# A Strassen down projection whose first two results reach x by a ScalarE copy and a transfer, with norm combinations split later and transposes moved

## The chip, the cores and the metric

The kernel runs on one core of one Trainium2 chip. The metric is device microseconds of that core. The kernel before takes 1888.84 us (median of 3 runs, 1888.61 to 1888.88).

## The reference, cut to what matters

A trunk of two layers on a float32 x of 512 positions by 1024 channels:

```
def swiglu(h, w_gu, w_down):                       # w_gu 1024 x 2*2816, w_down 2816 x 1024
    g, u = jnp.split(h @ w_gu, 2, axis=-1)
    return (jax.nn.silu(g) * u) @ w_down

for l in range(2):
    x = x + 0.5 * swiglu(rmsnorm(x, ln_ffn1[l]), w_ffn1_gu[l], w_ffn1_down[l])
    h = rmsnorm(x, ln_mix[l])
    z = h @ w_in[l]                                # pool input, q, k, v, gate logits
    a = pool_mixer(...) @ w_pool_branch[l]
    b = sliding_window_attention(...) @ w_attn_branch[l]
    x = x + (sigmoid(gp) * a + sigmoid(ga) * b) @ w_out[l]
    x = x + 0.5 * swiglu(rmsnorm(x, ln_ffn2[l]), w_ffn2_gu[l], w_ffn2_down[l])
```

All of it is float32. The change lies in the four SwiGLU blocks and at their borders to the mixers.

## The kernel before, in words

**Precision.** A float32 operand is split in two parts of a rounded type that TensorE takes at full rate: the high part is a copy by ScalarE, the low part is the operand less the high one, by VectorE. A product is then three matmuls (high by high, high by low, low by high). So every weight and every activation needs one pass of ScalarE and one of VectorE before TensorE can use it. `split` does both at once. `halve` issues the copy at once and leaves the subtraction on a list, `unsettled`, which the next call of `settle` issues.

**Strassen.** The products of an FFN are cut in 2 by 2 blocks and computed as seven products instead of eight, in the order a11, s1, s2, a12, s3, s4, a22 (`ORDER`). Three PSUM tiles hold the results, called by their role: a11, s2, s3 and a22 accumulate one upon the other in A, s1 and s4 in C, a12 in Dd. After each product a step reads what has accumulated so far. The factors of s1 to s4 are sums and differences: of weights they are made in SBUF, or by a second DMA that accumulates (issued by GpSimd, so on the queue that the page calls POOL's; the first DMA is issued by SyncE); of activations they are made by VectorE.

**FFN.** The 2816 hidden channels are worked off in three groups: 768 (2 x 384), 1024 and 1024 (2 x 512) in the very first FFN, with the 768 in the middle in the other three. A group is two `block`s (gate and up projection, i = 0 and 1, of width n) and one `down` (back to 1024 channels, added into x). That makes 12 downs. The last of each FFN is called final; with three of the four a norm `nxt` follows, and the last one of all writes the output. A product in a block or a 512-wide down is 24 matmuls in four quarters (c, q) of six, c the weight tile, q one of two row tiles. In a 384-wide down the second weight tile has half the matmuls, 18 in all.

**Order of the work.** All engines are wrapped so that each one's queue is the order in which the program was written (`InOrder`); nothing is scheduled by a planner. What goes between the quarters of a product is written in a dictionary `mid`: the entry (kind, c, q) runs after that quarter, behind a `settle`. After the first weight tile and after each product's step comes `W.prep`, which issues on VectorE and ScalarE the low part, sum and high part of the weights some 3 or 4 tiles ahead (tiles `wl`, `sums`, `wh`, from 7 buffers `raw`) and the loads that have become possible.

**Down.** Each step adds its share into a quarter of x, by a VectorE operation that reads PSUM: two row halves by two column halves (`add(t, d, c)`). The shares of a11 and a12 go into the same quarter, as do those of s1 and s3, and of s2 and s4. The operands of the next products are made between: `high(name)` is ScalarE's copy, `low(name)` VectorE's subtraction, `ops["t4"]` a combination of the last block's transposed result, still in PSUM, with the tile `fa`; fa is then the source of a22's operand. `flush` issues the transposes of the last block's result. In a final down `whole` has ScalarE sum the squares of the x that is complete, and `nxt.feed(q, i, bank)` has TensorE transpose a quarter of x and ScalarE scale it and take its high part.

**Norm.** For the FFN that follows, the class `Norm` makes the factors of the Strassen block from the transposed x: `t1` to `t4` are the combinations (tiles `more` in the trace, `xgh` and `xgl` where they share the place of the plain parts), each a VectorE operation on 128x512 and then a `split`. What isn't done by the end of the producer is kept on a list (`left`, `pend`), and `due` issues one of its steps in a hook of the first block of the FFN: t3 twice, t2 twice, feed(2) and feed(3), t3_split twice, t4 twice. A norm for the mixer (`halves` false) has only the feeds.

**Mixer.** Its first work is `begun`: two tiles `late` (PSUM) take the first half of the first two weight tiles' terms, then after a `settle` the feeds that were left and the q, k, v products follow.

The hooks of an FFN's first block, before:

```
mid = {at: due for at in (
    ("a11", 0, 0), ("a11", 0, 1), ("s1", 0, 0), ("s1", 0, 1), ("a12", 0, 0), ("a12", 0, 1),
    ("s3", 0, 1), ("s3", 1, 1),
)}
mid["s1", 1, 1] = lambda: due(turn[:, 0, :])
mid["s2", 0, 1] = lambda: due(roles[2][:, 0, :])
```

Of the kernel before, what the change touches and what calls it, by code (L numbers as in the profile page):

```python
# [13 lines left out]
AF = mybir.ActivationFunctionType  # L14
ALU = mybir.AluOpType
# [5 lines left out]
S = 512  # L21
# [87 lines left out]
def trunk(ctx, tc, x0, xT, consts, vecs, rows, w_g4, w_g3, w_d8, w_d6, w_qkv, w_u, w_pool, w_gate, w_br, w_out, out):  # L109
# [204 lines left out]
    def term(pt, i, n, wh, wl, ah, al):  # L314
        nc.tensor.matmul(pt, wh, ah, start=i == 0, stop=False)
        nc.tensor.matmul(pt, wh, al, start=False, stop=False)
        nc.tensor.matmul(pt, wl, ah, start=False, stop=i == n - 1)
# [30 lines left out]
    class Norm:  # L348
# [61 lines left out]
        def t1(self, j):  # L410
            d = temp("d")
            nc.vector.tensor_tensor(out=d, in0=self.keep[0, j], in1=self.keep[1, j], op=ALU.subtract)
            split(*self.both(T1, j), d)

        def t3(self, j):
            self.keep[4, j] = t = self.place(1, 2, j, F32)
# [2 lines left out]
        def t2(self, j):  # L419
            t = self.keep[0, j]  # L420
            nc.vector.scalar_tensor_tensor(
                out=t, in0=t, scalar=-1.0, in1=self.keep[4, j], op0=ALU.mult, op1=ALU.subtract
            )
            split(*self.both(T2, j), t)

        def t3_split(self, j):
            split(*self.both(T3, j), self.keep[4, j])

        def t4(self, j):
            u = temp("t4")  # L430
            nc.vector.scalar_tensor_tensor(
                out=u, in0=self.keep[0, j], scalar=-1.0, in1=self.keep[3, j], op0=ALU.mult, op1=ALU.subtract
            )
            split(*self.both(T4, j), u)

        def first(self, j, src, scale):
            d = temp("d")[:, :HT]
# [80 lines left out]
    def due(bank=None):  # L518
        if pend:
            pend.pop(0)(bank)  # L520
# [9 lines left out]
    def ffn(ctx, nm, nxt, last):  # L530
# [129 lines left out]
        def low(name):  # L660
            ops.pop((name, "low"))()
# [103 lines left out]
        def down(n, final):  # L765

            jn = n // P

            def add(t, d, c):
                def go(pt):  # L770
                    y = x[:, 2 * t:2 * t + 2, d * S:(d + 1) * S]
                    nc.vector.scalar_tensor_tensor(out=y, in0=pt, scalar=c, in1=y, op0=ALU.mult, op1=ALU.add)
                return go

            def whole(t, d, qs=range(2)):
                if not final:
                    return
                for q in qs:
                    b = 2 * t + q
                    if last:  # L780
                        nc.sync.dma_start(
                            out=out[b * P:(b + 1) * P, d * S:(d + 1) * S], in_=x[:, b, d * S:(d + 1) * S]
                        )
                    else:
                        nxt.squares(d, b)

            def a11(pt):
                add(0, 0, 0.5)(pt)
                return flush

            def s1(pt):
                add(1, 1, -0.5)(pt)
                nc.vector.tensor_tensor(out=f["b"], in0=f["c"], in1=f["b"], op=ALU.subtract)

            def s2(pt):
                add(1, 0, 0.5)(pt)
                low("s3")

            def a12(pt):
                add(0, 0, 0.5)(pt)  # L800
                ops.pop("t4")()
                whole(0, 0)

            def s3(pt):
                add(1, 1, -0.5)(pt)
                low("a22")
                whole(1, 1)

            def s4(pt):
                add(1, 0, 0.5)(pt)  # L810
                whole(1, 0)
                if final:
                    W.sums = None

            def a22(pt):
                y = x[:, 0:2, S:2 * S]
                for q in range(2):
                    nc.vector.scalar_tensor_tensor(
                        out=y[:, q, :], in0=pt[:, q, :], scalar=-0.5, in1=y[:, q, :], op0=ALU.mult, op1=ALU.add
                    )  # L820
                    whole(0, 1, [q])

            mid = {
                ("a11", 1, 0): lambda: low("s2"), ("s1", 0, 1): lambda: low("a12"),
                ("s2", 0, 1): lambda: high("s3", f["b"], n), ("a12", 0, 1): lambda: high("s4", f["c"], n),
                ("s3", 0, 0): lambda: low("s4"), ("s3", 0, 1): lambda: high("a22", f["a"], n),
            }
            if final and nxt is not None:
                spot = [t[:, 0, :] for t in (roles[2], turn)]
                feed = lambda q, t, at: lambda: nxt.feed(q, t, spot[at])  # L830
                mid.update({
                    ("s3", 1, 0): feed(0, 0, 0), ("s3", 1, 1): feed(1, 0, 1), ("s4", 0, 1): feed(2, 1, 0),
                    ("s4", 1, 1): feed(3, 1, 1), ("a22", 0, 1): feed(0, 1, 0), ("a22", 1, 0): feed(1, 1, 1),
                })
                if nxt.halves:
                    mid["a22", 1, 1] = lambda: [nxt.t1(j) for j in range(2)]
                left(nxt)

            strassen(
                ORDER, S, (2, jn - 2), lambda kind, k, q: [ops[kind][:, i, q, k * P:(k + 1) * P] for i in range(2)],  # L840
                dict(a11=a11, s1=s1, s2=s2, a12=a12, s3=s3, s4=s4, a22=a22), mid,
            )

# [5 lines left out]
        for gi, (_, group) in enumerate(groups(nm is first)):  # L849
            for i, n in enumerate(group):  # L850
                if nm is first and gi == i == 0:
                    plain(n, xt, acc, later)
                else:
                    mid = {}
                    if nm is first:
                        if gi == 0:
                            mid["s1", 1, 1] = flush
                    elif gi == i == 0:
                        mid = {at: due for at in (
                            ("a11", 0, 0), ("a11", 0, 1), ("s1", 0, 0), ("s1", 0, 1), ("a12", 0, 0), ("a12", 0, 1),  # L860
                            ("s3", 0, 1), ("s3", 1, 1),
                        )}
                        mid["s1", 1, 1] = lambda: due(turn[:, 0, :])
                        mid["s2", 0, 1] = lambda: due(roles[2][:, 0, :])
                    block(n, i, ORDER, mid)
            down(n, gi == 2)

    @with_exitstack
    def mix(ctx, l, nm, nxt):
# [225 lines left out]
        late = [mm() for _ in range(2)]  # L1095
        w = [W.take("u") for _ in range(2)]

        def begun(h):
            for i in range(2):
                for k, t in enumerate(nm.terms(w[i])[4 * h:4 * h + 4]):  # L1100
                    term(late[i], 4 * h + k, KT, *t)
                if h:
                    W.prep()

        begun(0)
        settle()
        due(side_bank[0])
        for q, width in ((False, 256), (True, 512)):
            pts = [t[:, :width] for t in (mm(), mm(), wide[:, 0, :], wide[:, 1, :])]
            per = CH // width  # L1110
            for c in range(KT // per):
                w_ = W.take("qkv")
                for b in range(NB):
                    for k in range(per):
                        kt, cols = per * c + k, slice(k * width, (k + 1) * width)
                        rows = slice(b % 2 * P, (b % 2 + 1) * P)
                        term(
                            pts[b], kt, KT, *(t[:, kt // 2, b // 2, kt % 2, rows] for t in (nm.h, nm.l)),
                            w_[0][:, cols], w_[1][:, cols],
                        )  # L1120
                    if not q and c == 0 and b == 1:
                        settle()
                        due(side_bank[1])
                    if not q and c == 1 and b == 1:
                        nm.spread(side_bank[1])
                        for i in range(2):
                            pooled(i, late[i])
                if not q and c == 0:
                    settle()
                    nm.sums()  # L1130
                    praw = temp("praw")
                    nc.sync.dma_start(out=praw, in_=w_pool[l])
                    begun(1)
                if c + 1 < KT // per:
                    W.prep()
                if q and c == 1:
                    side(-2)
            for b in range(NB):
                nc.scalar.activation(
                    out=(qs[b] if q else kv[:, b]).rearrange("p h d -> p (h d)"),  # L1140
                    in_=pts[b], func=AF.Copy, scale=nm.rstd[:, b:b + 1],
                )
            W.prep()
            if not q:
                split(*spare[4], praw)
            side(-1 if q else -3)
# [196 lines left out]
```

## Time and profile before

| | |
|---|---|
| runs, median (lowest to highest) | 1888.84 us (1888.61 to 1888.88) |
| profiled execution | 1888.9 us, span 1887.0 us |
| TensorE busy | 1858.3 us, 98% |
| VectorE / ScalarE / GpSimd busy | 1448.5 / 1008.6 / 124.5 us |
| granted TensorE clock | 0.999 |
| DMA, mean over the span | 155 GB/s |

The profile page is one execution. The span runs from its first to its last recorded instruction; the profiled execution's time is slightly longer. PE is TensorE's matmul side, PEld its weight loads, DVE VectorE, ACT ScalarE, POOL GpSimd, SP SyncE. A row of a listing by instruction gives the start in us, the duration, the engine, the line, the operation, output and input by the program's names, the shapes, and in brackets how long the engine had been idle before it and what it had been waiting for. `mm` is a PSUM tile of results, `pt` the PSUM tile of transposed results, `op` an operand of a down, `xg`, `xgh` and `xgl` the scaled transposed x and its parts, `r`, `p`, `u`, `fa`, `fb`, `fc` intermediate results of a block. Since the wrapper records every operation, nearly all have line 97; they are told apart by tiles.

### The profile page before, as it was taken

The numbers are of one execution on the slowest core, as the hardware profiler recorded it, in microseconds if no ns is written. First come the engines' busy times: TensorE is split into PE (matmuls) and PEld (weight loads), VectorE is DVE, ScalarE is ACT, GpSimd is POOL, SyncE is SP. The second block draws the span as 40 slices with busy tenths as digits, with TensorE's granted clock in tenths as the row PEclk, the third lists the DMA queues.
The fourth block names the chain that finished last, engine by engine and source line by source line (L and its number), as shares of the span: only waits on it lengthen the run. The fifth ranks groups of instructions, "written<-read, shape, count | busy, mean of one in ns | idle before, by whom it ended". The sixth has DMA issues, their size and how long they took to land.

```text
span 1887.0 us, 23912 instructions
## 1 busy us (share of the span) xinstructions
PE 1858.3 (98%) x8928; PEld 1555.4 (82%) x8928; DVE 1448.5 (77%) x1829; ACT 1008.6 (53%) x1493; POOL 124.5 (7%) x152
## 2 busy tenths in 40 slices
PE   9999999999999999999999999999999999999998
PEld 8888888887788788988878898888877887899887
DVE  7878878677564988887988878786675648888878
ACT  6555455645454654555665555555554446545553
POOL 0100000000000001110001001100000000001000
PEclk9999999999999999999999999999999999999999
DMA  8687666322223676777657667753212237667763
GB/s 251 179 229 180 193 174 171 125 80 77 79 89 101 166 199 161 183 204 188 170 158 196 157 179 206 191 166 107 90 68 90 93 86 203 171 168 184 218 179 100
DMA packets 87571, 292.80 MB, mean 155 GB/s; under 512 B 9856, under 2 KB 10112, under 8 KB 87456
## 3 DMA queue, kind: packets, MB, share of 16 engines
q1 hardware_dynamic: 67104, 223.47, 35.1%
q0 software_dynamic: 20208, 67.78, 20.4%
q8 instruction: 70, 1.15, 0.2%
q14 instruction: 45, 0.37, 0.1%
q10 hardware_dynamic: 144, 0.03, 0.0%
HBM read 289.15 MB, written 2.10 MB: 154 GB/s over the span
## 4 chain that ended last, share of the span: by engine, by line
PE 80%; DVE 12%; ACT 6%; issue 1%; DMA 1%; SPq 0%; DVEq 0%; ACTq 0%
PE mm L97 73%; DVE wl L97 4%; PE sc L97 4%; DVE sums L97 2%; PE pt L97 2%; ACT wh L97 2%; PE pt_pv L97 1%; DVE x L97 1%; DVE more L97 1%; ACT xgh L97 1%; DVE op L97 1%; ACT xg L97 1%; PE pt_tp L97 1%; DVE fa L97 1%; ACT sq L97 1%
## 5 line engine op out<-in xcount | busy, mean ns | idle before, releaser
L97 ACT CAST wh<-raw 128x1024 fp32r<-128x1024 f32 (+3 forms) x443 | 432.9, 988 | 274.9 <-PE mm L97 197.0
L97 DVE TENSOR_TENSOR wl<-raw,wh 128x1024 fp32r<-128x1024 f32 (+3 forms) x443 | 502.2, 1146 | 90.5 <-PE mm L97 57.8
L97 PE MATMUL mm<-wh,op 128*128 128x512 f32 x1232 | 392.1, 394 | 2.4 <-DVE op L97 2.4
L97 PE MATMUL mm<-wh,more 128*128 128x512 f32 (+1 forms) x1104 | 335.2, 374 | 3.8 <-ACT more L97 2.6
L97 PE MATMUL mm<-wl,xgh 128*128 128x512 f32 (+2 forms) x840 | 310.4, 370 | 5.9 <-DVE wl L97 5.6
L97 PE MATMUL mm<-wh,xgh 128*128 128x512 f32 (+2 forms) x840 | 312.2, 372 | 1.3 <-ACT xg L97 0.8
L97 PE MATMUL mm<-wh,xgl 128*128 128x512 f32 (+2 forms) x840 | 309.8, 369 | 0.9 <-DVE xgl L97 0.9
L97 PEld LDWEIGHTS mm<-wh,op 128*128 128x128 f32 x1232 | 230.6, 188 | 52.4 <-DVE op L97 5.8
L97 PE MATMUL mm<-wl,op 128*128 128x512 f32 x616 | 240.3, 390 | 1.6 <-DVE wl L97 1.6
L97 PEld LDWEIGHTS mm<-wh,more 128*128 128x128 f32 x1104 | 204.7, 188 | 36.8 <-ACT more L97 3.3
L97 PE MATMUL mm<-wl,more 128*128 128x512 f32 (+1 forms) x552 | 206.6, 374 | 1.7 <-DVE wl L97 1.7
L97 DVE TENSOR_TENSOR wl<-sums,wh 128x1024 fp32r<-128x1024 f32 (+1 forms) x140 | 159.0, 1137 | 45.0 <-ACT wh L97 28.7
L97 ACT CAST wh<-sums 128x1024 fp32r<-128x1024 f32 (+1 forms) x140 | 136.2, 981 | 95.0 <-DVE sums L97 52.2
L97 PEld LDWEIGHTS mm<-wl,xgh 128*128 128x128 f32 x840 | 157.9, 188 | 31.1 <-DVE wl L97 10.3
L97 PEld LDWEIGHTS mm<-wh,xgh 128*128 128x128 f32 x840 | 157.8, 188 | 23.5 <-ACT xg L97 2.1
L97 PEld LDWEIGHTS mm<-wh,xgl 128*128 128x128 f32 x840 | 157.8, 188 | 23.2 <-DVE xgl L97 2.1
L97 POOL DMA_DIRECT2D raw<-in_w_g x92 | 79.5, 864 | 1325.5 <-DMA raw<-in_w_g 591.6
L97 PEld LDWEIGHTS mm<-wl,op 128*128 128x128 f32 x616 | 115.8, 188 | 26.2 <-DVE wl L97 3.3
L97 PE MATMUL mm<-xgh,wh 128*128 128x512 f32 x320 | 129.4, 404 | 0.4 <-ACT xgh L97 0.4
L97 PE MATMUL mm<-xgl,wh 128*128 128x512 f32 x320 | 125.3, 392 | 0.4 <-DVE xgl L97 0.4
L97 PE MATMUL mm<-xgh,wl 128*128 128x512 f32 x320 | 125.2, 391 | 0.0
L97 PEld LDWEIGHTS mm<-wl,more 128*128 128x128 f32 x552 | 103.6, 188 | 18.5 <-DVE wl L97 3.3
(247 smaller groups left out, 2397.7 us busy)
## 6 DMA issues: line engine op xcount, KB each, us to landing
raw<-in_w_g SPq DMA_DIRECT2D x160, 512.0 KB, 5.0
raw<-in_w_d SPq DMA_DIRECT2D x100, 512.0 KB, 4.5
raw<-in_w_g POOLq DMA_DIRECT2D x64, 512.0 KB, 6.9
raw<-in_w_g SPq DMA_DIRECT2D x77, 384.0 KB, 4.3
raw<-in_w_d POOLq DMA_DIRECT2D x40, 512.0 KB, 5.5
raw<-in_w_gate SPq DMA_DIRECT2D x32, 512.0 KB, 3.2
raw<-in_w_g POOLq DMA_DIRECT2D x28, 384.0 KB, 5.8
raw<-in_w_br SPq DMA_DIRECT2D x16, 512.0 KB, 3.2
```

Of the source, the lines that this page charges most:

```text
L97: return lambda *args, **kw: self.tc.keep_in_program_order(call(*args, **kw))
```

## The change

In every down the shares of a11 and s1 are no longer added into x by VectorE. `aside` has ScalarE copy them out of PSUM, scaled, into an SBUF tile (`p` or `u`, both free at that time), and `gathered` issues a GpSimd DMA that accumulates the tile into x, one in the second quarter of s1 and one in the second quarter of s2. Around that, in the down, the low part of s4's operand moves from the first quarter of s3 into the step of a12, t4 from the step of a12 to the first quarter of s3, a22's high part from the second to the third quarter of s3, and its low part from the step of s3 to the first quarter of s4. In the final downs the feeds move: feed(0, 0) a quarter earlier, feed(2, 1) two quarters later.

In `Norm`, t1, t2, t3_split and t4 end in `halve` in place of `split`. In the first block of an FFN the steps that were due at (s1, 0, 1), (s1, 1, 1) and (s2, 0, 1) come a quarter earlier or more: one at (a11, 1, 0), feed(2) at (s1, 1, 0), feed(3) at (s2, 0, 0). In the mixer the first four terms of both tiles still run before the settle, but in two pieces: terms 0 and 1 of the one tile and of the other, then terms 2 and 3; before, four terms of the one tile were followed by four of the other.

```diff
--- before.py
+++ after.py
@@ -410,7 +410,7 @@
         def t1(self, j):
             d = temp("d")
             nc.vector.tensor_tensor(out=d, in0=self.keep[0, j], in1=self.keep[1, j], op=ALU.subtract)
-            split(*self.both(T1, j), d)
+            halve(*self.both(T1, j), d)
 
         def t3(self, j):
             self.keep[4, j] = t = self.place(1, 2, j, F32)
@@ -421,17 +421,17 @@
             nc.vector.scalar_tensor_tensor(
                 out=t, in0=t, scalar=-1.0, in1=self.keep[4, j], op0=ALU.mult, op1=ALU.subtract
             )
-            split(*self.both(T2, j), t)
+            halve(*self.both(T2, j), t)
 
         def t3_split(self, j):
-            split(*self.both(T3, j), self.keep[4, j])
+            halve(*self.both(T3, j), self.keep[4, j])
 
         def t4(self, j):
             u = temp("t4")
             nc.vector.scalar_tensor_tensor(
                 out=u, in0=self.keep[0, j], scalar=-1.0, in1=self.keep[3, j], op0=ALU.mult, op1=ALU.subtract
             )
-            split(*self.both(T4, j), u)
+            halve(*self.both(T4, j), u)
 
         def first(self, j, src, scale):
             d = temp("d")[:, :HT]
@@ -784,12 +784,23 @@
                     else:
                         nxt.squares(d, b)
 
+            def aside(t, d, c, pt, name):
+                half = wide(name)
+                nc.scalar.activation(out=half, in_=pt, func=AF.Copy, scale=c)
+                pend_x.append((x[:, 2 * t:2 * t + 2, d * S:(d + 1) * S], half))
+
+            def gathered():
+                y, half = pend_x.pop(0)
+                nc.gpsimd.dma_start(out=y, in_=half, accum_op=ALU.add)
+
+            pend_x = []
+
             def a11(pt):
-                add(0, 0, 0.5)(pt)
+                aside(0, 0, 0.5, pt, "p")
                 return flush
 
             def s1(pt):
-                add(1, 1, -0.5)(pt)
+                aside(1, 1, -0.5, pt, "u")
                 nc.vector.tensor_tensor(out=f["b"], in0=f["c"], in1=f["b"], op=ALU.subtract)
 
             def s2(pt):
@@ -798,12 +809,11 @@
 
             def a12(pt):
                 add(0, 0, 0.5)(pt)
-                ops.pop("t4")()
+                low("s4")
                 whole(0, 0)
 
             def s3(pt):
                 add(1, 1, -0.5)(pt)
-                low("a22")
                 whole(1, 1)
 
             def s4(pt):
@@ -821,15 +831,16 @@
                     whole(0, 1, [q])
 
             mid = {
-                ("a11", 1, 0): lambda: low("s2"), ("s1", 0, 1): lambda: low("a12"),
-                ("s2", 0, 1): lambda: high("s3", f["b"], n), ("a12", 0, 1): lambda: high("s4", f["c"], n),
-                ("s3", 0, 0): lambda: low("s4"), ("s3", 0, 1): lambda: high("a22", f["a"], n),
+                ("a11", 1, 0): lambda: low("s2"), ("s1", 0, 1): lambda: [low("a12"), gathered()],
+                ("s2", 0, 1): lambda: [high("s3", f["b"], n), gathered()], ("a12", 0, 1): lambda: high("s4", f["c"], n),
+                ("s3", 0, 0): lambda: ops.pop("t4")(), ("s3", 1, 0): lambda: high("a22", f["a"], n),
+                ("s4", 0, 0): lambda: low("a22"),
             }
             if final and nxt is not None:
                 spot = [t[:, 0, :] for t in (roles[2], turn)]
                 feed = lambda q, t, at: lambda: nxt.feed(q, t, spot[at])
                 mid.update({
-                    ("s3", 1, 0): feed(0, 0, 0), ("s3", 1, 1): feed(1, 0, 1), ("s4", 0, 1): feed(2, 1, 0),
+                    ("s3", 0, 1): feed(0, 0, 0), ("s3", 1, 1): feed(1, 0, 1), ("s4", 1, 0): feed(2, 1, 0),
                     ("s4", 1, 1): feed(3, 1, 1), ("a22", 0, 1): feed(0, 1, 0), ("a22", 1, 0): feed(1, 1, 1),
                 })
                 if nxt.halves:
@@ -857,11 +868,11 @@
                             mid["s1", 1, 1] = flush
                     elif gi == i == 0:
                         mid = {at: due for at in (
-                            ("a11", 0, 0), ("a11", 0, 1), ("s1", 0, 0), ("s1", 0, 1), ("a12", 0, 0), ("a12", 0, 1),
+                            ("a11", 0, 0), ("a11", 0, 1), ("a11", 1, 0), ("s1", 0, 0), ("a12", 0, 0), ("a12", 0, 1),
                             ("s3", 0, 1), ("s3", 1, 1),
                         )}
-                        mid["s1", 1, 1] = lambda: due(turn[:, 0, :])
-                        mid["s2", 0, 1] = lambda: due(roles[2][:, 0, :])
+                        mid["s1", 1, 0] = lambda: due(turn[:, 0, :])
+                        mid["s2", 0, 0] = lambda: due(roles[2][:, 0, :])
                     block(n, i, ORDER, mid)
             down(n, gi == 2)
 
@@ -1095,14 +1106,16 @@
         late = [mm() for _ in range(2)]
         w = [W.take("u") for _ in range(2)]
 
-        def begun(h):
+        def begun(ks):
             for i in range(2):
-                for k, t in enumerate(nm.terms(w[i])[4 * h:4 * h + 4]):
-                    term(late[i], 4 * h + k, KT, *t)
-                if h:
+                terms = nm.terms(w[i])
+                for k in ks:
+                    term(late[i], k, KT, *terms[k])
+                if ks[-1] == KT - 1:
                     W.prep()
 
-        begun(0)
+        begun((0, 1))
+        begun((2, 3))
         settle()
         due(side_bank[0])
         for q, width in ((False, 256), (True, 512)):
@@ -1130,7 +1143,7 @@
                     nm.sums()
                     praw = temp("praw")
                     nc.sync.dma_start(out=praw, in_=w_pool[l])
-                    begun(1)
+                    begun((4, 5, 6, 7))
                 if c + 1 < KT // per:
                     W.prep()
                 if q and c == 1:
```

## The prediction

> **What bounds the kernel now.** I read the cores first, then the busy times, then busy time by stretch, then who waits for whom in the stretches that fall short.
>
> ```profile
> core 0: 1887.0 us, clock 0.999
> ```
> ```profile
> PE 1858.3 (98%) x8928; PEld 1555.4 (82%) x8928; DVE 1448.5 (77%) x1829; ACT 1008.6 (53%) x1493; POOL 124.5 (7%) x152
> ```
>
> TensorE runs at full clock and is busy for all but 28.7 us. That understates its stalls, since a matmul's end is modelled. The weight loads (PEld) are the finer measure. Columns of the next rows: the stretch, its length, then PE, PEld, DVE, ACT and POOL busy (with counts), the clock, the DMA share, GB/s. The first is undisturbed, the second the first block of layer 0's second FFN, the third the last down before layer 1's first FFN with that FFN's first block.
>
> ```profile
> 230.00:240.00 10.00, 10.00 (x46) 8.29 (x45) 4.87 (x4) 6.01 (x6) 0.42 (x2) 1.00 0.75 227
> 609.05:654.80 45.75, 42.50 (x187) 32.63 (x186) 39.77 (x56) 30.74 (x44) 2.66 (x4) 1.00 0.56 150
> 926.95:993.00 66.05, 61.70 (x279) 48.10 (x278) 58.23 (x76) 45.91 (x77) 5.18 (x6) 1.00 0.64 172
> ```
>
> Undisturbed, PEld is busy 0.829 of the time and a 512-wide matmul comes every 10/45 = 0.22 us (0.227 between starts). At that rate the second stretch lost 45.75 - 32.63/0.829 = 6.4 us and the third 66.05 - 48.10/0.829 = 8.0 us. VectorE is busy for 87% of the second. So where TensorE waits, it waits for VectorE and ScalarE queues, which run in program order. Who waits, in the second stretch (total us, times, longest), TensorE first:
>
> ```profile
> PEld mm L97 <- DVE wl L97: 2.9, 4, 0.9
> PEld mm L97 <- ACT more L97: 0.9, 1, 0.9
> PEld mm L97 <- ACT wh L97: 0.8, 1, 0.8
> PEld mm L97 <- DVE xgl L97: 0.7, 1, 0.7
> PEld mm L97 <- ACT xg L97: 0.7, 1, 0.7
> PEld mm L97 <- DVE more L97: 0.7, 2, 0.4
> ```
> ```profile
> DVE more L97 <- ACT more L97: 3.2, 4, 1.1
> ```
>
> The last row is the handle: VectorE, behind with its work, sits idle 3.2 us inside split, waiting for ScalarE's high part before it subtracts the low one.
>
> **The change part by part.**
>
> *The offload.* In each of 12 downs two VectorE adds leave and two ScalarE copies come, plus two accumulating transfers on POOL's queue.
>
> ```profile
> L97 DVE SCALAR_TENSOR_TENSOR x<-mm,x x96: 681/1218/1225, 81.8 to 1883.0; 128x1024 f32<-128x1024 f32 x72, 128x512 f32<-128x512 f32 x24
> ```
> ```profile
> L97 ACT COPY p<-mm x23: 793/1007/1019, 56.9 to 1815.6; 128x1024 f32<-128x1024 f32 x16, 128x768 f32<-128x768 f32 x7
> ```
>
> That is 24 x 1.22 = 29 us off VectorE and 24 x 1.01 = 24 us onto ScalarE (53% busy). What does it bring? VectorE in a 512-wide down, from the add of s2:
>
> ```profile
> 712.20 1.23 DVE L97 SCALAR_TENSOR_TENSOR x<-mm,x 128x1024 f32<-128x1024 f32 x1 [0.81 <-PE mm L97]
> ...
> 719.01 1.22 DVE L97 SCALAR_TENSOR_TENSOR x<-mm,x 128x1024 f32<-128x1024 f32 x1
> 720.15 1.21 DVE L97 SCALAR_TENSOR_TENSOR fa<-fa,pt 128x1024 f32<-128x1024 f32 x1
> 721.28 1.22 DVE L97 TENSOR_TENSOR wl<-sums,wh 128x1024 fp32r<-128x1024 f32 x1
> 722.41 1.22 DVE L97 TENSOR_TENSOR op<-fc,op 128x1024 fp32r<-128x1024 f32 x1
> ```
>
> Before s2's add VectorE already waits 0.81 us for TensorE. The adds taken away lie ahead of that wait, so they lengthen it; all that follows stays where it is. I take 0 us for the offload (ends: 0, and a gain of 2 x 1.22 for a down whose queue is late there). ScalarE's copies stand where it has slack, and bank A is next written one product (24 matmuls, 5.4 us) later; price 0. Without that cover each copy would cost about 1 us.
>
> *s4's low part before t4.* TensorE's stalls at the start of s4, first and last of their kinds:
>
> ```profile
> 98.01 0.19 PEld L97 LDWEIGHTS mm<-wl,op 128*128 128x128 f32 x1 [0.83 <-DVE wl L97]
> 98.88 0.30 PEld L97 LDWEIGHTS mm<-wh,op 128*128 128x128 f32 x2 [0.68 <-DVE op L97]
> ...
> 214.59 0.30 PEld L97 LDWEIGHTS mm<-wh,op 128*128 128x128 f32 x2 [0.61 <-DVE op L97]
> ...
> 1871.56 0.30 PEld L97 LDWEIGHTS mm<-wh,op 128*128 128x128 f32 x2 [0.61 <-DVE op L97]
> ```
>
> Now s4's low part runs directly after a12's add: at 720.2 instead of 722.4, before s4 begins. The weight's wl at 721.28 keeps its place. Five 512-wide downs (214.59 to 1871.56) gain 0.5 each, 2.5 us. In four 384-wide ones (98 to 1756) only the second wait goes, the wl wait stays, and a22's low part, now queued behind one wl more, takes some back: 0.4 each, 1.6 us.
>
> *The final downs' transposes.* feed(2,1) asks for an x that s3's add has not written, because that add is queued behind a low part that waits for ScalarE. From the waits of the last down before layer 1, and of the one before layer 0's mix:
>
> ```profile
> PEld mm L97 <- ACT xgh L97: 1.5, 1, 1.5
> ```
> ```profile
> PEld mm L97 <- ACT xgh L97: 2.1, 2, 1.5
> PEld mm L97 <- DVE xgl L97: 0.8, 2, 0.5
> ```
>
> A quarter product (1.36 us) later, that x is there. What is late next: feed(1) waits about 0.2 us for the t4 that now reads PSUM later, and feed(0,1) about 0.6 us for s4's add. So TensorE leaves the down 1.0 us earlier. ScalarE, saturated there, does not get faster: the mix then waits for its first operand, and begun in four pieces gives it 12 matmuls to do where there were 6. Walking both queues, the 13th matmul of the mix starts 1.15 us earlier. Two such places: 2.3 us.
>
> *Splits into halves, and t2 and the feeds one step earlier,* in three first blocks. VectorE and TensorE in the second stretch:
>
> ```profile
> 622.14 0.19 PEld L97 LDWEIGHTS mm<-wh,more 128*128 128x128 f32 x1 [0.94 <-ACT more L97]
> ...
> 648.66 0.19 PEld L97 LDWEIGHTS mm<-wl,more 128*128 128x128 f32 x1 [0.89 <-DVE wl L97]
> ```
> ```profile
> 634.98 1.29 DVE L97 TENSOR_TENSOR more<-more 128x512 fp32r<-128x512 f32 x2
> 636.18 1.22 DVE L97 TENSOR_TENSOR wl<-raw,wh 128x1024 fp32r<-128x1024 f32 x1
> 637.32 1.22 DVE L97 TENSOR_TENSOR sums<-sums,raw 128x1024 f32<-128x1024 f32 x1
> 638.45 1.22 DVE L97 TENSOR_TENSOR r<-r,mm 128x1024 f32<-128x1024 f32 x1
> ```
>
> The 3.2 us of idling go. Two things come: the low part of feed(2) finds VectorE waiting for ScalarE some 0.6 us longer, and T3's second low part, now done at 634.98, moves behind wl, sums and r's add, 3 x 1.14 = 3.4 us. By my walk it ends at 638.6 when TensorE wants it at 637.3, a new stall of 1.3 us in the second half of s3. T4's two waits vanish behind it, so a22 finds its weights and starts at 646.4, where the old one got going at 648.4 (648.66 less one matmul). Gain 2.1 us, in both second FFNs: 4.2. In the third stretch the queue is late from the start, t1's two waits go as well and TensorE brings 1.0 us along: a22 at 983.4 against 986.8, 3.4 us.
>
> *The new wait.* a12's add must now wait for a transfer issued behind POOL's own weight addition. POOL and VectorE in a 512-wide and a 384-wide down, and the landing of POOL's additions (min, median, max):
>
> ```profile
> 707.61 0.87 POOL L97 DMA_DIRECT2D raw<-in_w_g  x1 [8.10 <-DMA raw<-in_w_g]
> ```
> ```profile
> 804.30 0.87 POOL L97 DMA_DIRECT2D raw<-in_w_g  x1 [2.03 <-DVE wl L97]
> ```
> ```profile
> 813.30 1.22 DVE L97 SCALAR_TENSOR_TENSOR x<-mm,x 128x1024 f32<-128x1024 f32 x1
> ```
> ```profile
> DMA to landing us min/median/max: 4.2/5.9/10.8
> ```
>
> POOL is free at 708.5 and the add is due at 719.0: 10.5 us. In the 384-wide down, 805.2 to 813.3: 8.1 us. A transfer within SBUF does not occur in this trace; the nearest row gives 5.9 us, inside both. Behind a late add everything on VectorE slips one for one. Ends: 0, and at 10.8 us 4 x 2.7 + 4 x 0.3 = 12 us. I take 0.3 for each 384-wide down, 1.2 us.
>
> Sum: 2.5 + 1.6 + 2.3 + 4.2 + 3.4 - 1.2 = 12.8 us, against the profiled execution's 1888.9 us (span 1887.0; median of the runs 1888.84): 1876 us.
>
> A rule that speaks against the change: the Trainium skill, "SBUF — State Buffer", section "SBUF: two separate sides", holds that a DMA issued from GpSimd can starve, since its descriptors are not written while VectorE holds the shared port in a two-port mode. Here POOL's issue took 0.87 us both at 707.61 and at 804.30 with VectorE busy, so this trace does not show it; by the rule the transfers would land late, and the time would be that of the first rival. The same skill's "DMA: Bandwidth & Descriptors", section "Anatomy of one DMA", gives about 2.0 us plus bytes/436e3, an estimate of 3.2 us for 512 KB; the measured median is 5.9. By it the 1.2 us fall away: 1875 us.
>
> **The rivals.**
> *The transfer is late* (slower). If it takes over L us from POOL's turn to land, the cost is 4(L - 8.1) + 4(L - 10.5); it eats the 14.0 us at L = 11.05. At 13 it is 30 us: 1905. For it: two transfers follow each other and weight loads run beside them. Against: the median of 5.9. Final downs have far more time. Chance 0.12, starved descriptors 0.03 of it.
> *The blocks give nothing back:* VectorE, 87% busy, loses at T3 and feed(2) what the splits free. Then 7.6 us go: about 1883.5. For it: my walk leaves 1.3 us of new stall. Against: 3.2 us of idling removed from the late engine. Chance 0.17.
> *The offload does pay:* the queue keeps its lead past s2's add, the wl wait at 98.01 (0.83) goes too and the blocks give a little more: 4 x 0.7 and 3 us more, 1870. Against: the 0.81 us wait at 712.20. Chance 0.11.
>
> **How the numbers follow.** The forecast, 1871 to 1881, has 0.60. The range 1869 to 1886 leaves out the late transfer and little else. A measurement of this kernel can tell about 0.2%, 3.8 us, from no change. Faster by more than that: the forecast, the offload that pays and most of the blocks' case, 0.80; within it 0.09 (the poor end of that case, a transfer slightly late); slower 0.11.
>
> **What would show it.** VectorE's idle time before s2's add should grow beyond 0.81 us; the waits of TensorE for op at s4 should be gone and the 0.83 for wl stay; the 1.5 us at feed(2,1) should be gone; VectorE's waits for ScalarE's more should nearly vanish, with a new TensorE wait for the low part of T3; a12's adds should show no wait for a DMA, or a short one in the 384-wide downs. Transfers that land after 8 to 10 us, or a wait of a12's add above 1 us in every down, would make the prediction wrong.

## The result and the profile after

The changed kernel takes 1876.48 us (median of 4 runs, 1876.08 to 1877.06), the kernel before, beside it, 1888.72 us (1888.13 to 1888.88). The ratio is 0.9936, with a 95% interval of 0.9919 to 0.9953: 12.2 us faster, where 12.8 had been forecast (1876). The profiled execution's span went from 1887.0 to 1874.3 us. First its cores and its busy times:

```profile
core 0: 1874.3 us, clock 1.000
```
```profile
PE 1854.3 (99%) x8928; PEld 1556.8 (83%) x8928; DVE 1421.7 (76%) x1805; ACT 1029.8 (55%) x1517; POOL 152.0 (8%) x176
```

VectorE lost 24 instructions and 27 us, ScalarE gained 24 and 21 us, POOL gained 24 instructions. TensorE has the same 8928 matmuls at the same clock (0.999 before): what went is waiting. Next the two stretches of the prediction, at the same instructions but for the first, which begins 0.4 us earlier here (length, then PE, PEld, DVE, ACT, POOL busy, clock, DMA share, GB/s):

```profile
606.30:650.66 44.36, 42.05 (x190) 33.07 (x189) 40.31 (x57) 30.64 (x44) 3.12 (x4) 1.00 0.58 154
921.95:985.05 63.10, 60.92 (x282) 48.36 (x280) 58.95 (x77) 46.07 (x77) 5.14 (x6) 1.00 0.68 180
```

By the undisturbed rate of 0.829 the first lost 44.36 - 33.07/0.829 = 4.5 us (6.4 before), the second 4.8 (8.0 before). From the block's first weight load to that of the next one, the first block itself went from 45.75 to 43.90 us. Who waits for whom in the first of them, TensorE's rows (total us, times, longest):

```profile
PEld mm L97 <- DVE more L97: 1.7, 2, 1.4
PEld mm L97 <- DVE wl L97: 1.7, 2, 0.9
...
PEld mm L97 <- DVE xgl L97: 0.7, 1, 0.7
PEld mm L97 <- ACT xg L97: 0.6, 1, 0.6
```

The waits for ScalarE's more and wh are gone and there were two fewer waits for wl. VectorE's wait for ScalarE inside split, 3.2 us before, has no row here any more. In its place stands the stall that was forecast at 1.3 us; VectorE's queue, and TensorE at s3's second half:

```profile
634.71 1.21 DVE L97 TENSOR_TENSOR r<-r,mm 128x1024 f32<-128x1024 f32 x1
635.84 0.68 DVE L97 TENSOR_TENSOR more<-more 128x512 fp32r<-128x512 f32 x1
```
```profile
636.57 0.30 PEld L97 LDWEIGHTS mm<-wh,more 128*128 128x128 f32 x2 [1.41 <-DVE more L97]
```

In the downs, VectorE's low part for a12, then its adds of s2 and a12, in a 512-wide one; then the two adds in a 384-wide one:

```profile
700.02 1.23 DVE L97 TENSOR_TENSOR op<-pt,op 128x1024 fp32r<-128x1024 f32 x1 [1.35 <-ACT op L97]
...
708.07 1.23 DVE L97 SCALAR_TENSOR_TENSOR x<-mm,x 128x1024 f32<-128x1024 f32 x1 [1.66 <-PE mm L97]
714.88 1.22 DVE L97 SCALAR_TENSOR_TENSOR x<-mm,x 128x1024 f32<-128x1024 f32 x1
...
803.17 1.23 DVE L97 SCALAR_TENSOR_TENSOR x<-mm,x 128x1024 f32<-128x1024 f32 x1 [0.84 <-PE mm L97]
...
808.65 1.22 DVE L97 SCALAR_TENSOR_TENSOR x<-mm,x 128x1024 f32<-128x1024 f32 x1
```

The wait before s2's add is longer (0.81 to 1.66), and a12's add waits for no transfer in any of the 12 downs. The 0.85 us are not all that was taken away: two adds, 1.14 us each from start to start, have gone from the queue. Most of the rest is the new wait of 1.35 us in the first row, for ScalarE's high part, which now stands behind the copy of a11's share in ScalarE's queue. So ScalarE's copies do hold VectorE up here; the kernel's time does not show it, since VectorE waits for TensorE behind that in any case. TensorE in a 384-wide down and around a final one:

```profile
97.81 0.19 PEld L97 LDWEIGHTS mm<-wl,op 128*128 128x128 f32 x1 [0.83 <-DVE wl L97]
102.41 0.30 PEld L97 LDWEIGHTS mm<-wh,op 128*128 128x128 f32 x2 [0.42 <-DVE op L97]
...
328.32 0.42 PEld L97 LDWEIGHTS mm<-cst,x 128*128 128x128 f32 x4 [0.39 <-DVE x L97]
331.73 0.42 PEld L97 LDWEIGHTS pt<-cst,x 128*128 128x128 f32 x4 [0.40 <-DVE fa L97]
341.73 0.42 PEld L97 LDWEIGHTS mm<-cst,x 128*128 128x128 f32 x4 [0.62 <-ACT xgh L97]
346.09 0.19 PEld L97 LDWEIGHTS mm<-xgl,wh 128*128 128x128 f32 x1 [0.54 <-DVE xgl L97]
```

At s4 the 0.83 for wl stayed, the waits for op are gone (no row in the 512-wide downs either), and TensorE waits 0.42 for a22's low part. The 1.5 us at feed(2, 1) became three small stalls. The transfers, with KB each and median us from issue to landing, and their issues on POOL in the 384-wide down:

```profile
x<-p POOLq DMA_DIRECT2D x12, 512.0 KB, 7.2
x<-u POOLq DMA_DIRECT2D x12, 512.0 KB, 8.6
```
```profile
800.46 1.53 POOL L97 DMA_DIRECT2D x<-p  x1
801.17 2.04 POOL L97 DMA_DIRECT2D x<-u  x1
```

From 800.46 to the add at 808.65 there were 8.2 us of room.

### The profile page after: what moved, and what is told of

The parts are those of the page before. It is cut to its first block, busy times and chain, and to the rows that moved or that the text cites. A ratio compares the mean times of both kernels' runs of the same rounds, so it can differ in the third digit from the quotient of the medians.

```text
span 1874.3 us, 23990 instructions
## 1 busy us (share of the span) xinstructions
PE 1854.3 (99%) x8928; PEld 1556.8 (83%) x8928; DVE 1421.7 (76%) x1805; ACT 1029.8 (55%) x1517; POOL 152.0 (8%) x176
## 4 chain that ended last, share of the span: by engine, by line
PE 84%; DVE 8%; ACT 5%; issue 2%; DMA 1%; SPq 0%; DVEq 0%; POOL 0%; ACTq 0%
PE mm L97 77%; PE sc L97 4%; DVE wl L97 2%; PE pt L97 2%; ACT wh L97 2%; DVE sums L97 1%; PE pt_pv L97 1%; DVE x L97 1%; DVE more L97 1%; ACT sq L97 1%; ACT xgh L97 1%; ACT xg L97 1%; PE pt_tp L97 1%; DVE xgl L97 0%; ACT s L97 0%
```

## The experiments

Twelve kernels, each timed in five rounds beside the kernel before, which took 1888.67 to 1888.89 us there; the changed kernel's 1876.48 is from its own comparison. The runs of one kernel lie within 1.7 us of each other, except where said. Expectations speak of theories by letter: A is always the prediction's way of reckoning, that a stall belongs to the place where an in-order queue is late.

**The four parts, undone one at a time.** First the offload:

```diff
-                aside(0, 0, 0.5, pt, "p")
+                add(0, 0, 0.5)(pt)
...
-                aside(1, 1, -0.5, pt, "u")
+                add(1, 1, -0.5)(pt)
...
-                ("s1", 0, 1): lambda: [low("a12"), gathered()],
-                ("s2", 0, 1): lambda: [high("s3", f["b"], n), gathered()],
+                ("s1", 0, 1): lambda: low("a12"),
+                ("s2", 0, 1): lambda: high("s3", f["b"], n),
```

> The changed kernel, but the shares of a11 and s1 are again added into x by VectorE; no copy by ScalarE, no transfer. Theory A (the prediction: the adds lie ahead of a wait for TensorE, so taking them away only lengthens that wait): same time as the changed kernel, 1876.5 us within 1 us, VectorE's wait before s2's add back from 1.67 to about 0.8 us in 512-wide downs and to 0 in 384-wide ones. Rival B (the offload pays because VectorE's queue keeps a lead through the rest of the down): 3 to 6 us slower than the changed kernel, 1879.5 to 1882.5. Rival C (the transfers cost something): up to 2 us faster than the changed kernel.

1876.09 us (1875.94 to 1876.92): the same as the changed kernel, by its own spread. The offload, as it stands in this change, brings nothing. Its trace has the two waits of the 384-wide down where they were:

```profile
812.29 0.19 PEld L97 LDWEIGHTS mm<-wl,op 128*128 128x128 f32 x1 [0.84 <-DVE wl L97]
816.89 0.30 PEld L97 LDWEIGHTS mm<-wh,op 128*128 128x128 f32 x2 [0.42 <-DVE op L97]
```

Second, the order in the downs:

```diff
                 add(0, 0, 0.5)(pt)
-                low("s4")
+                ops.pop("t4")()
...
                 add(1, 1, -0.5)(pt)
+                low("a22")
...
-                ("s3", 0, 0): lambda: ops.pop("t4")(), ("s3", 1, 0): lambda: high("a22", f["a"], n),
-                ("s4", 0, 0): lambda: low("a22"),
+                ("s3", 0, 0): lambda: low("s4"), ("s3", 0, 1): lambda: high("a22", f["a"], n),
```

(in the final downs a22's high part goes into the hook of feed(0, 0), ahead of it)

> The changed kernel with the old order in the downs: t4 in a12's step, s4's low part in the first quarter of s3, a22's high part in its second quarter, a22's low part in s3's step. Theory A (every stall belongs to its own place, the parts add up): 5 x 0.61 + 4 x 0.68 of waits at the start of s4 come back, 4 x 0.42 of the wait for a22's low part in the 384-wide downs go: 4.1 us slower than the changed kernel, 1880.6. Rival D (the offload's lead lets VectorE reach t4 and s4's low part earlier, so the old order costs nothing any more): 1876.5.

1881.15 us, 4.7 more (4.1 expected). Theory A; D is out, since the offload's lead does not reach s4. The old waits are back, first a 384-wide, then a 512-wide down:

```profile
99.36 0.30 PEld L97 LDWEIGHTS mm<-wh,op 128*128 128x128 f32 x2 [0.68 <-DVE op L97]
214.96 0.30 PEld L97 LDWEIGHTS mm<-wh,op 128*128 128x128 f32 x2 [0.61 <-DVE op L97]
```

Third, the norm: split for halve in t1, t2, t3_split and t4, and the old hooks.

> The changed kernel with the old norm: t1 to t4 with both parts split at once, and the old hooks of the first blocks. Theory A: the three first blocks lose what they gained, 1.6 to 2.1 in each second FFN and some 2.3 before layer 1, about 6 us: 1882.5. Rival E (the blocks are bound by VectorE's total work, and the gain seen there comes from work that arrives earlier because of the rest of the change): under 2 us, below 1878.5.

1883.24 us, 6.8 more (some 6 expected): theory A, the blocks' gain is the norm's own. Fourth, the feeds and begun:

```diff
-                    ("s3", 0, 1): feed(0, 0, 0), ("s3", 1, 1): feed(1, 0, 1), ("s4", 1, 0): feed(2, 1, 0),
+                    ("s3", 1, 0): lambda: [high("a22", f["a"], n), nxt.feed(0, 0, spot[0])], ("s3", 1, 1): feed(1, 0, 1), ("s4", 0, 1): feed(2, 1, 0),
...
-        begun((0, 1))
-        begun((2, 3))
+        begun((0, 1, 2, 3))
```

> The changed kernel with the transposes of the final downs and the start of the mixer in the old places. Theory A: the 1.5 us stall at feed(2, 1) comes back in three downs, and the three small stalls (0.39, 0.40, 0.62) go; net 0.9 us at each of the two places before a mixer and somewhat less before layer 1, where VectorE is the limit: 2 to 2.7 us, 1878.5 to 1879.2. Rival F (ScalarE's and VectorE's queues set the start of the next stage, whatever TensorE does before): 0.5 us or less, 1877.

1879.33 us, 2.9 more, just above the 2 to 2.7 of A; F is out. The four together are -0.4 + 4.7 + 6.8 + 2.9 = 14.0 us for a change worth 12.2: nearly additive. The 1.8 us over, more than the scatter of single runs, mean that some parts are worth more beside the others than alone; which, no run here shows, since no two of the four were undone together.

**Inside the norm's part.** Splits back, new hooks kept, then the old hooks with the halves:

```diff
-            halve(*self.both(T1, j), d)
+            split(*self.both(T1, j), d)
```

(and so in t2, t3_split and t4)

> The changed kernel with t1 to t4 split at once again (VectorE waits for ScalarE's high part each time), but with the new hooks of the first blocks. Theory A (the halves carry the gain, because VectorE's waits of 3.2 us in one block go): most of the 6.8 us that undoing both cost, some 4 us, comes back; less the 1.4 us stall at T3's second low part, which the split puts back ahead of wl: 1878.5 to 1881. Rival G (the earlier hooks carry it): 1876.5 or less, since T3's stall goes and nothing else returns.

1883.23 us. This missed the range that A had given: with splits the earlier hooks are worth nothing, since 1883.24 is what splits with the old hooks take. VectorE's 3.2 us of waiting are back, and TensorE's stalls in layer 0's block changed little but their names (0.57 and 1.07 at T2 where splits with the old hooks have 0.95, 0.43 and 0.19; at a22 0.81 and 0.89, where they have 0.78 and 0.89):

```profile
DVE more L97 <- ACT more L97: 3.2, 4, 1.1
```
```profile
619.50 0.19 PEld L97 LDWEIGHTS mm<-wh,more 128*128 128x128 f32 x1 [0.57 <-ACT wh L97]
620.75 0.19 PEld L97 LDWEIGHTS mm<-wl,more 128*128 128x128 f32 x1 [1.07 <-DVE wl L97]
...
645.48 0.19 PEld L97 LDWEIGHTS mm<-wh,more 128*128 128x128 f32 x1 [0.81 <-ACT wh L97]
646.55 0.19 PEld L97 LDWEIGHTS mm<-wl,more 128*128 128x128 f32 x1 [0.89 <-DVE wl L97]
```

```diff
-                            ("a11", 0, 0), ("a11", 0, 1), ("a11", 1, 0), ("s1", 0, 0), ("a12", 0, 0), ("a12", 0, 1),
+                            ("a11", 0, 0), ("a11", 0, 1), ("s1", 0, 0), ("s1", 0, 1), ("a12", 0, 0), ("a12", 0, 1),
...
-                        mid["s1", 1, 0] = lambda: due(turn[:, 0, :])
-                        mid["s2", 0, 0] = lambda: due(roles[2][:, 0, :])
+                        mid["s1", 1, 1] = lambda: due(turn[:, 0, :])
+                        mid["s2", 0, 1] = lambda: due(roles[2][:, 0, :])
```

> The changed kernel with the old hooks of the first blocks (t2's second, feed(2) and feed(3) a quarter or more later), the halves kept. Theory A (with the queues no longer stopped by the splits, the earlier feeds matter: a12 already waits 0.64 for xg, and a quarter is 1.36): up to 1.4 us in each of three blocks, 1877.5 to 1880.5. Rival L (the hooks are worth nothing, as the two runs with splits, alike to 0.01 us with old and new hooks, suggest): 1876.5 within 0.5.

1879.10 us: with halves the hooks are worth 2.6. T2's two waits return, in place of the 0.78 for wl that the changed kernel has there:

```profile
620.67 0.19 PEld L97 LDWEIGHTS mm<-wh,more 128*128 128x128 f32 x1 [0.94 <-ACT more L97]
621.40 0.30 PEld L97 LDWEIGHTS mm<-wh,more 128*128 128x128 f32 x2 [0.43 <-DVE more L97]
```

So the halves alone bring 1883.24 - 1879.10 = 4.1 us, the hooks on top 2.6; hooks without halves 0. An earlier place in a queue that then stops for another engine gains nothing.

Then the one split whose price the prediction had foreseen:

```diff
         def t3_split(self, j):
-            halve(*self.both(T3, j), self.keep[4, j])
+            split(*self.both(T3, j), self.keep[4, j])
```

> The changed kernel with T3 alone split at once again. Theory A (the new stall of 1.4 us in the second half of s3 is the price of moving T3's second low part behind wl, sums and r's addition, and nothing else waits there): it goes in three first blocks, 4.2 us: 1872.3. Rival K (VectorE has no slack up to a22's weights, so most of the stall comes back as a wait for wl at a22): 0.3 to 0.7 each, 1874.3 to 1875.6.

1875.19 us, 1.3 less, 0.43 for each block: K. The 1.41 us stall is gone, and this one, which the changed kernel has not, stands at a22:

```profile
644.30 0.19 PEld L97 LDWEIGHTS mm<-wl,more 128*128 128x128 f32 x1 [1.10 <-DVE wl L97]
```

**begun alone** (its two lines as above, the feeds kept):

> The changed kernel with the mixer's first eight terms in the old order (four of the one tile, then four of the other). Theory A: the wait for the high part of feed(1, 1), 0.62 before, comes back at both mixers, and the 0.54 for its low part stays: 0.6 each, 1877.7. Rival M (ScalarE's queue sets when the mixer gets going, the order of the terms does not matter): 1876.5.

1878.31 us, 1.8 more, 0.9 at each mixer (0.6 expected). So 1.8 of the 2.9 us of the fourth part are the order of the mixer's terms. The waits at its start, 0.54 alone in the changed kernel, are three:

```profile
346.41 0.19 PEld L97 LDWEIGHTS mm<-xgl,wh 128*128 128x128 f32 x1 [0.54 <-DVE xgl L97]
348.02 0.19 PEld L97 LDWEIGHTS mm<-xgh,wh 128*128 128x128 f32 x1 [0.61 <-ACT xgh L97]
348.74 0.19 PEld L97 LDWEIGHTS mm<-xgl,wh 128*128 128x128 f32 x1 [0.54 <-DVE xgl L97]
```

**The transfer made late.** A copy of one column of p onto itself, by VectorE behind s2's add, holds the first transfer back:

```diff
             def s2(pt):
                 add(1, 0, 0.5)(pt)
+                t = pend_x[0][1][:, 0, 0:1]
+                nc.vector.tensor_copy(out=t, in_=t)
+                gathered(0)
                 low("s3")
...
-                ("s1", 0, 1): lambda: [low("a12"), gathered()],
+                ("s1", 0, 1): lambda: low("a12"),
```

(gathered takes the place in the list that it is to issue, by default the last)

> The changed kernel with the first transfer held back: it is issued only once VectorE has passed s2's add, by a copy of one column of its source onto itself there; the second transfer goes first. Theory A (a late transfer delays a12's add, and everything on VectorE behind it one for one): issued at 709.4 and 804.4 in the downs whose a12 adds now start at 714.9 and 808.7, and landing 7.2 us later (the median of these transfers), it makes a12's add wait 1.7 us in a 512-wide down, 3.0 in a 384-wide one and about 1.5 in a final one; 4 x 6.2 = 25 us, less what stalls behind them absorb: 1892 to 1902. If they land 5 us after their issue, only the 384-wide downs wait, 0.8 each: 1880. Rival H (VectorE has slack behind a12's add): the wait shows in the records, the time stays below 1880.

1901.75 us (1896.81 to 1904.85, a wide scatter): slower than the kernel before. The size is the expected one, its make-up is not. A 512-wide and a 384-wide down, first the transfer's issue on POOL in the latter:

```profile
812.96 1.19 POOL L97 DMA_DIRECT2D x<-p  x1 [1.55 <-DVE p L97]
```
```profile
723.49 1.23 DVE L97 SCALAR_TENSOR_TENSOR x<-mm,x 128x1024 f32<-128x1024 f32 x1 [0.53 <-DMA x<-p]
822.40 1.23 DVE L97 SCALAR_TENSOR_TENSOR x<-mm,x 128x1024 f32<-128x1024 f32 x1 [5.40 <-DMA x<-p]
```
```profile
825.68 0.29 PEld L97 LDWEIGHTS mm<-wl,op 128*128 128x128 f32 x1 [6.38 <-DVE wl L97]
```

The 512-wide down waits 0.53 (1.7 expected), the 384-wide one 5.40 (3.0 expected), since there the transfer took from 812.96 to 822.40, 9.4 us; why it took that long no run shows. VectorE's wait reaches TensorE whole: 6.38 in place of 0.83. (This is the longest; TensorE's stalls for wl in the four 384-wide downs are 5.22, 6.38, 4.37 and 2.96.) And it costs more than that, by the granted clock (the last column but two) around that stall:

```profile
820.00:825.60 5.60, 0.00 (x0) 0.00 (x0) 3.20 (x4) 0.00 (x0) 0.87 (x1) 0.88 1.05 351
825.60:827.60 2.00, 1.92 (x5) 1.53 (x6) 2.00 (x4) 1.07 (x2) 0.00 (x0) 0.50 0.75 147
827.60:829.60 2.00, 2.00 (x6) 1.61 (x5) 2.00 (x3) 0.28 (x1) 0.00 (x0) 0.50 0.04 8
829.60:831.60 2.00, 2.00 (x7) 1.53 (x6) 1.32 (x2) 0.78 (x1) 0.00 (x0) 0.64 0.53 168
831.60:833.60 2.00, 2.00 (x11) 1.62 (x10) 1.24 (x2) 1.32 (x2) 0.00 (x0) 1.00 0.81 262
```

For some 5.5 us after it TensorE ran at half its clock, 5 to 7 matmuls in 2 us where there are later 11.

**The wait put to use.** If what the offload frees is lost ahead of s2's add, work that stood behind that add must gain from being moved ahead of it. s3's low part can go, since its high part is made two quarters earlier:

```diff
             def s2(pt):
                 add(1, 0, 0.5)(pt)
-                low("s3")
...
-                ("s4", 0, 0): lambda: low("a22"),
+                ("s4", 0, 0): lambda: low("a22"), ("s2", 1, 1): lambda: low("s3"),
```

> The changed kernel, but s3's low part is done right before the add of s2 (hook (s2, 1, 1)) and not behind it. Theory A (what the offload frees is lost as waiting before s2's add, 0.84 us in a 384-wide down and 1.67 in a 512-wide one, because nothing else stands there): the low part fills that wait, all of VectorE's queue behind it moves up by 0.84 and 1.14 us, so the waits at s4 (0.83 for wl) and at a22 (0.42 for op) of the four 384-wide downs go, 5.0 us, and of the three stalls of the final downs (0.39, 0.40, 0.62) those that VectorE ends, up to 0.8 in three places: 1869 to 1871.5. Rival I (the lead is used up by some other wait before s4, or the a12 add then waits for its transfer): 1875 or more.

1870.34 us (1869.51 to 1870.57), 6.1 less than the changed kernel: theory A. VectorE has no wait before s2's add, and all behind it is early (compare 806.35 - 801.74 with the 5.5 us between the same adds above):

```profile
800.82 0.95 DVE L97 TENSOR_TENSOR op<-fb,op 128x768 fp32r<-128x768 f32 x1
801.74 1.23 DVE L97 SCALAR_TENSOR_TENSOR x<-mm,x 128x1024 f32<-128x1024 f32 x1
...
806.35 1.22 DVE L97 SCALAR_TENSOR_TENSOR x<-mm,x 128x1024 f32<-128x1024 f32 x1
```
```profile
814.23 0.30 PEld L97 LDWEIGHTS mm<-wh,op 128*128 128x128 f32 x2 [0.26 <-DVE op L97]
```

The 0.83 for wl is gone in that down, 0.26 is left at a22, and in the final downs the 0.39, 0.40 and 0.62 are gone. In one of the four 384-wide downs 0.51 of the wait for wl stays, and there part of rival I shows:

```profile
1139.34 1.22 DVE L97 SCALAR_TENSOR_TENSOR x<-mm,x 128x1024 f32<-128x1024 f32 x1 [0.46 <-DMA x<-p]
```

The transfer was issued at 1131.97, so with the earlier queue its room of 8.2 us is down to 6.9, and that was not enough. The control is the same move without the offload:

> The same move of s3's low part, without the offload (the shares of a11 and s1 are added by VectorE). Theory A: in a 384-wide down VectorE has no wait before s2's add then, so the move only swaps two operations and nothing is gained; in a 512-wide one 0.8 of the 1.14 us is hidden, of use in the final downs alone: 1874.5 to 1876.5, that is 4 to 6 us behind the same kernel with the offload. Rival J (the place of the low part is all, the offload plays no part): the same time as with the offload.

1873.82 us (1873.40 to 1874.00). In the 384-wide downs nothing is gained, as expected:

```profile
811.54 0.19 PEld L97 LDWEIGHTS mm<-wl,op 128*128 128x128 f32 x1 [0.84 <-DVE wl L97]
816.14 0.30 PEld L97 LDWEIGHTS mm<-wh,op 128*128 128x128 f32 x2 [0.42 <-DVE op L97]
```

In the final downs the move by itself ends the three stalls, so it gains 2.3 us, 0.7 more than expected at best. With the move the offload is worth 1873.82 - 1870.34 = 3.5 us, less than the 4 to 6 that A expected; without it, nothing. J is out.

**The best version** has the offload and the move of s3's low part (1870.34), T3 split at once, and this, for an FFN's first block (the norm's sum is taken out of s2's step):

```diff
             def a12(pt):
+                if not early and not held:
+                    held.append(pt)
+                    return
...
             def s4(pt):
                 u, v = tile_["u"], tile_["p"]
+                if held:
+                    nm.sums()
+                    a12(held[0])
```

(`early` says that the norm's sum is already there)

> The changed kernel with s3's low part ahead of s2's add in the downs (1870.3 by itself), T3 split at once, and in the first block of an FFN the norm's sum and inverse root (12 small operations, 2.8 us), r's addition and its Silu moved from the steps of s2 and a12 to the step of s4. Theory A (the stalls left in the first blocks, 0.80 for xgl, 0.28 and 1.41 for more, are all VectorE's queue, and 4 us of it need not stand there): 2 to 2.5 us in each of three blocks: 1863 to 1865. Rival N (what is moved is late at the end of the block instead, or ScalarE's waits take over): 1867 to 1870.

1867.57 us (1866.71 to 1868.34), ratio to the kernel before 0.9889, 0.9875 to 0.9902: faster than the kernel before and the changed one by 21 and 9 us, but only 2.8 beyond the move of s3's low part, where A had 5 to 7; the time lies in rival N's range. The three stalls that were aimed at (0.80, 0.28 and 1.41 in layer 0's block with that move alone) are gone, those of 0.77 at s2 and 0.64 at a12 stay, and at the block's end TensorE now waits for p, 0.79 and 0.24, behind the moved operations, as N had it. What the later sums bring without T3's split was not run. The first of the two new waits:

```profile
647.65 0.42 PEld L97 LDWEIGHTS pt<-cst,p 128*128 128x128 f32 x4 [0.79 <-DVE p L97]
```

## Why the prediction was right

The sum was right to 0.6 us, and each gain came by the mechanism that was given for it. That it came so close is luck: 1.2 us were set aside for a wait that did not come, and the other terms came out about as much smaller. Read off the two traces, from weight load to weight load, they brought 3.9, 2.5 and 6.4 us, where 4.1, 3.3 and 6.6 had been forecast; 12.8 together, of a span that is 12.7 shorter.

- *The offload, 0.* Shown: undoing it changes the time by 0.4 us, within the scatter. The reason given, the wait before s2's add, is shown too, by filling that wait; part of what was freed is lost before that, in the wait for ScalarE (1.35 us above), whose copies the prediction had priced at 0. But 0 belongs to this order of the queue, not to the offload: the rival that priced the wl wait at 0.7 in each 384-wide down had the right place, and lacked only the move.
- *s4's low part, 2.5 + 1.6 = 4.1.* In the traces 0.5 for each 512-wide down and 0.34 for each 384-wide one, 3.9. Undone: 4.7. The waits went where they were said to go, the wl wait stayed, and a22 took back 0.42 in the 384-wide downs.
- *Final downs to mixers, 2.3, and 1.0 in the third stretch, 3.3.* Undone: 2.9. The stall of feed(0, 1) was put at 0.6 and measured 0.62; that of feed(1) at 0.2 and measured 0.40; that of feed(0, 0), 0.39, was missed. So the three new stalls are nearly as long as the 1.5 us that went, and TensorE leaves the down before layer 1 0.5 us earlier (from its first weight load to the first behind it, 904.07 to 947.19 before, 899.07 to 941.65 now), not 1.0; the prediction's own 1.5, less 0.2 and 0.6, gives 0.7. The other two final downs gained 0.4 each and the mixers behind them some 0.6 each, 2.0 for the 2.3. (feed(2, 1) moved one quarter, as the prediction has it and the diff shows, not the two that the description of the change names.) Of the 2.9 us, 1.8 are the mixer's order of terms, undone alone, so the transposes, which the text put first, carry the smaller share.
- *The first blocks, 2 x 2.1 and the rest of the third stretch's 3.4.* The stretches lost 1.9 and 3.3 us less than before (the prediction: 2.1 and 3.4); the block alone makes 1.9 of the one and 2.7 of the other. Undone, the norm's part costs 6.8 against 4.2 + 2.4. T3's new stall came at 1.41 for 1.3, and a22 started without a wait.
- *The new wait, 1.2 to pay.* This term was wrong: nothing waits for a transfer. It was taken from a nearest row of 5.9 us, and the transfers take 7.2 and 8.6; x<-p, for which a12's add would wait, is in time with 7.2 for a room of 8.2 us in the 384-wide down. The rival of the late transfer was no straw man: issued some 4 us later against the adds (4.0 us of room in the 384-wide down, 812.96 to 817.00, where there were 8.2), it lost 25 us.

On this last point the Trainium skill, "DMA: Bandwidth & Descriptors", section "Anatomy of one DMA", gives a fit from which 3.2 us for 512 KB is an estimate; the trace has 7.2 and 8.6 for these transfers, which add to x and run beside weight loads. The Trainium skill, "SBUF — State Buffer", section "SBUF: two separate sides", warns that VectorE, in a two-port mode, keeps such a DMA's descriptors from being written; POOL's issues took 1.2 to 2.0 us, the long ones back to back with another, against 0.85 for the weights', and no wait followed in the changed kernel, so no run here shows starving.

What the sum didn't see is what a stall is worth. It reckoned T3's 1.3 as paid and the a22 waits as gone because of it, which was right; but undoing T3 alone gave back 0.43 of 1.41, since another wait, 1.10 us for wl, then comes up at a22.

## What to carry to other kernels

Taking work off a late in-order engine gains nothing where the engine then waits for something else before its next instruction: look in the trace for the first wait behind what was removed, and move into it an operation that stands behind it. A split that makes one engine wait for another in the middle of its queue delays all that is queued behind it; issue the first half, and the second when the first is surely done. Price a stall by what is late next, not by its own length.

## What the runs showed of the hardware

After TensorE's weight loads had stood still for 6.38 us, its granted clock was 0.50 for some 5 us (rows above), and it was 0.50 behind a stall of 2.96 in another 384-wide down of the same run, while behind one of 1.16 us it was 1.00:

```profile
1674.50:1676.50 2.00, 1.94 (x8) 1.61 (x9) 2.00 (x3) 0.83 (x1) 0.00 (x0) 1.00 0.97 180
```
```profile
1769.80:1771.80 2.00, 1.97 (x5) 1.60 (x6) 2.00 (x3) 1.13 (x2) 0.00 (x0) 0.50 1.09 338
```

So the one-for-one price of a late add, which the prediction used for its slower rival, holds here for the short stalls only; for one of 6.38 us half of the 5 us at half clock comes on top, an estimate of 2.5 us. The Trainium skill, "TensorE: Matmul & The Clock Gate", "Part 1: The HAM clock gate", has the half clock after an idle window of some 3.4 us; here a stall of 2.96 was enough. The longest stalls of TensorE's weight loads in the kernels before and after are 1.52 and 1.46 us, and both run at a clock of 0.999 and 1.000; no run here has a stall between 1.6 and 2.9 us.
